# Down projection of a SwiGLU block moved to its own stage, sixteen of its inner tiles as seven block products

## The chip, the cores and the metric

The kernel runs on one core of one Trainium2 chip. The metric is the device time of one execution in microseconds (us), lower is better. A program on one core has TensorE (PE in the profile; PEld is its weight load), VectorE (DVE), ScalarE (ACT), GpSimd (POOL) and a sync engine (SP), which here issues every DMA. Each engine works through its own list of instructions in order and waits on semaphores for the others.

## The reference, cut to what matters

One layer on 1024 tokens of width 1024: a mixer (spatial gating, convolution module, gated delta rule), its output projection with a residual, and then a gated feed-forward part, which is what the change touches:

```python
x = x + jnp.einsum("bte,ed->btd", mix, w_out[l])
h = rms_norm(x, ffn_norm_g[l])
ff = jax.nn.silu(jnp.einsum("btd,df->btf", h, w_gate[l])) * jnp.einsum("btd,df->btf", h, w_up[l])
x = x + jnp.einsum("btf,fd->btd", ff, w_down[l])
return rms_norm(x, final_norm_g)
```

The inner width is 2816, which is 22 tiles of 128; all values are 32-bit floats.

## The kernel before, in words

Everything lies transposed: channels in the 128 partitions, tokens along the row, in two halves of 512. A product of 32-bit numbers is done in three passes: each operand is split into a high part (an ACT cast) and the rest (a DVE subtraction), and high x high, high x low and low x high are summed in PSUM (`PASSES`; `split_w` L126, `split` L85, `split_b` L705). So one tile of 128 x 128 weights against 512 tokens is three matmuls, and each split is one ACT and one DVE instruction of 128x512.

Gate and up (`class Matrix`, L804): two output tiles of a matrix at a time, over all eight contraction tiles. The four blocks of the weights and the four blocks of the activations (contraction halves by token halves) are combined so that seven block products take the place of eight. Each block product is 4 contraction tiles x 3 passes = 12 matmuls of 512 columns. The sums of weights, s1 to s3, are made on POOL (L832 to L843) and split as w6, w5, w7, w4, w3; w1 and w2 are plain. The sums of the activations, T1 to T4, and the plain block B22 are made once, ahead of the stage, from `b0` and `b1` on DVE and POOL. Products accumulate in two or three PSUM tiles: X takes w1, w6, w7, w4 in that order and is copied out between them (c11, c12, c22), Y takes w2, Z takes w5 and w3. The 22 matrices run as g0, u0, g1, u1, ... in `seq` (L881); the next one's w1 and w2 products stand between the present one's w7 and its w4.

Down (`class Downs`, L966): gate times up of a pair of tiles is split at once (`up_out`, L948) and kept in SBUF. After every second pair the four tiles that have come together are multiplied with all of their `w_down` rows: 16 products (8 output tiles x 2 token halves) of 4 tiles x 3 passes = 12 matmuls each, PSUM tile `pd`. Each is added to the residual: load a tile of `X1d` from DRAM into `xa`, add on DVE (L982), store it again. This is done for groups 0 to 3, tiles 0 to 15. The last six tiles (`LAST` = 20 here marks the last two of them) are multiplied at the end, PSUM tile `pdl`, with the final norm behind it in pieces of 512, 256 and 256 tokens.

Order: the program text gives each instruction a priority, and the framework's scheduler builds one fixed list per engine from it when the kernel is compiled; slots of a pool (`raw` has 2 for loaded weights, the high and low parts 6 each, `kq` 4, `d` 50) are handed out in that order and make the waits. At run time nothing is reordered. DMAs go over eight lanes in turn, and SP waits for an issue whose lane is busy, or whose data is not ready, with all later ones behind it.

Of the kernel before, what the change touches and what calls it, by code (L numbers as in the profile page):

```python
# [16 lines left out]
P = 128  # L17
# [3 lines left out]
KT = 8  # L21
# [16 lines left out]
def tile_kernel(ctx: ExitStack, tc: tile.TileContext, xT, wt, wub, wv, wout, wg, wu, wd, wdl,  # L38
# [160 lines left out]
    def token_sums(parts, w, name):  # L199
        # sum over the channels, each token in a partition  # L200
# [165 lines left out]
    # sums of the decays along the rows, each on all partitions in turn  # L366
# [46 lines left out]
    # inverses of the 32 x 32 diagonal blocks, one block to a partition  # L413
# [42 lines left out]
    def prep(c):  # L456
# [10 lines left out]
        # M' = M - M L M over pairs of 32 x 32 blocks, then of 64 x 64 blocks  # L467
# [44 lines left out]
    for c in range(NC):  # L512
# [29 lines left out]
        # the output takes the place of the chunk's queries  # L542
# [66 lines left out]
    def gating():  # L609
# [119 lines left out]
    def token_scale(ps, w, name):  # L729
        # the scale of each token, along the rows  # L730
# [66 lines left out]
    # blocks: contraction halves by token halves; T1 = B12 - B11, T2 = B22 - T1, T3 = B22 - B12, T4 = B21 - T2  # L797
# [6 lines left out]
    class Matrix:  # L804
        """Columns f and f + 1 of one of the two matrices: rows A11 A12 and A21 A22."""

        def __init__(self, src, f, name):
            self.src, self.f, self.name, self.row = src, f, name, {}
# [52 lines left out]
        def product7(self):  # L861
            product(self.X, self.w7, T3, False, False)
# [4 lines left out]
        def end(self):  # L867
            product(self.X, self.w4, T4, False, True)
            product(self.Z, self.w3, B22, False, True)
            DVE.tensor_tensor(self.c12, self.Z, self.c12, op=ALU.add)  # L870

        def product3(self):
            self.W = misc(f"W{self.name}")
            product(self.W, self.w3, B22, True, True)

        def end4(self):
            product(self.X, self.w4, T4, False, True)
# [3 lines left out]
    seq = [Matrix(src, 2 * p, f"{n}{p}") for p in range(FT // 2) for src, n in ((wg, "g"), (wu, "u"))]  # L881
# [40 lines left out]
    B22 = [block([c4p.tile([P, 2, H], F32R, tag="c4", name=f"B22{i}{j}") for j in range(2)]) for i in range(2)]  # L922
    for k in range(HB):
# [4 lines left out]
    T3 = [block([cvp.tile([P, 2, H], F32R, tag="cv", name=f"T3h{i}") for i in range(2)]),  # L928
          block([cvp.tile([P, 2, H], F32R, tag="cv", name="T3l")]) + [dt(f"T3l{k}", F32R) for k in range(2)]]
# [10 lines left out]
    ff = {}  # L940

# [6 lines left out]
    def up_out(g, u):  # L948
# [4 lines left out]
        for i, hf, t in ((0, 0, g.c11), (1, 1, g.c22), (1, 0, g.c21), (0, 1, g.c12)):  # L953
            ff[f + i, hf] = split(t, f"ff{f + i}{hf}")
# [8 lines left out]
    def group_terms(gi, n, wtile):  # L963
# [205 lines left out]
```

## Time and profile before

| | us |
|---|---|
| median of three runs | 1181.55 |
| lowest and highest | 1180.44, 1182.04 |
| profiled execution, span from the first to the last instruction | 1181.6 |
| PE busy | 1154.2 (98%) |
| DVE busy | 725.5 (61%) |
| ACT busy | 453.3 (38%) |
| POOL busy | 261.9 (22%) |

The page gives no other time of the profiled execution than its span. "Busy" adds up the time in which an engine has an instruction in work. Matmuls overlap each other, so the time from one to the next is shorter than the mean time of one. The granted clock of PE is 2.4 GHz over nearly all of the span (mean 0.994).

### The profile page before, as it was taken

The page shows a single profiled execution, that of the slowest core. Times are in us where ns is not written, and L with a number is a line of the kernel's source. Part 1 is how long each engine was busy: PE and PEld are TensorE (multiplying, and loading weights), DVE is VectorE, ACT ScalarE, POOL GpSimd, SP SyncE. Part 2 cuts the span into 40 slices and gives each one's busy share as a digit, 9 for nine tenths or more (in the row PEclk, how much of TensorE's full clock was granted, in tenths as well). Part 3 has the DMA queues.
Part 4 walks back from the last instruction along what each step waited for, and adds up shares of the span by engine and source line. Part 5 has one row for each costly group of instructions (what it writes and reads, how often), then busy time and mean ns, then how long its engine had stood idle before and what let it go on. Part 6 is the DMA issues. An engine that isn't in the chain of part 4 may idle for free.

```text
span 1181.6 us, 15892 instructions
## 1 busy us (share of the span) xinstructions
PE 1154.2 (98%) x5974; PEld 952.9 (81%) x5974; DVE 725.5 (61%) x1168; ACT 453.3 (38%) x959; POOL 261.9 (22%) x212
## 2 busy tenths in 40 slices
PE   8999999999899999979999999999999999999997
PEld 6889888888688778858888888888888888888797
DVE  7699879868987657596533654355326542645523
ACT  7456561224235654445311432144204420433422
POOL 3000130010613221564110321032004201332042
PEclk9999999999999999989999999999999999999999
DMA  6235343453313455403255125512552145215312
GB/s 227 62 98 179 108 134 102 129 193 115 131 48 107 143 174 172 144 19 106 78 182 169 59 67 172 180 58 72 165 190 74 59 134 199 81 36 182 103 58 87
DMA packets 76813, 141.68 MB, mean 120 GB/s; under 512 B 15264, under 2 KB 27200, under 8 KB 76736
## 3 DMA queue, kind: packets, MB, share of 16 engines
q1 hardware_dynamic: 76736, 140.66, 36.4%
q8 instruction: 47, 0.77, 0.3%
q14 instruction: 30, 0.25, 0.1%
HBM read 102.35 MB, written 38.29 MB: 119 GB/s over the span
## 4 chain that ended last, share of the span: by engine, by line
PE 89%; DVE 5%; issue 1%; DMA 1%; POOL 1%; ACT 1%; SPq 0%; POOLq 0%; DVEq 0%; ACTq 0%
PE pd L959 15%; PE Xu L801 10%; PE Xg L801 9%; PE po L726 7%; PE pdl L959 5%; PE Zu L801 5%; PE Zg L801 4%; PE pv L227 4%; PE pq L227 4%; PE pk L227 3%; PE pg L227 2%; PE Yu L801 2%; PE Yg L801 2%; PE pu L305 2%; PE pv L602 2%
## 5 line engine op out<-in xcount | busy, mean ns | idle before, releaser
L982 DVE TENSOR_TENSOR xa<-pd,xa 128x512 f32<-128x512 f32 x64 | 44.3, 692 | 115.1 <-PE pd L959 112.7
L959 PE MATMUL pd<-ff_l,wd_h 128*128 128x512 f32 x256 | 101.1, 395 | 0.0
L959 PE MATMUL pd<-ff_h,wd_l 128*128 128x512 f32 x256 | 101.1, 395 | 0.0
L959 PE MATMUL pd<-ff_h,wd_h 128*128 128x512 f32 x256 | 100.9, 394 | 0.0
L663 DVE SCALAR_TENSOR_TENSOR ca<-cy,vec,ca 128x512 f32<-128x512 f32 x120 | 93.1, 798 | 0.5
L832 POOL TENSOR_TENSOR s1u<-u_r 128x512 f32<-128x512 f32 x11 | 19.3, 1752 | 186.4 <-DMA u_r<-in_wu_dram 186.4
L959 PEld LDWEIGHTS pd<-ff_h,wd_h 128*128 128x128 f32 x256 | 48.2, 188 | 11.5
L959 PEld LDWEIGHTS pd<-ff_l,wd_h 128*128 128x128 f32 x256 | 48.1, 188 | 11.4
L959 PEld LDWEIGHTS pd<-ff_h,wd_l 128*128 128x128 f32 x256 | 48.1, 188 | 11.3
L843 POOL TENSOR_TENSOR s2u<-u_r,s2u 128x512 f32<-128x512 f32 x11 | 18.5, 1681 | 145.9 <-DVE w6u_l L130 145.9
L129 ACT CAST wd_h<-wd_r 128x512 fp32r<-128x512 f32 x38 | 23.4, 620 | 63.2 <-PE pd L959 24.9
L130 DVE TENSOR_TENSOR wd_l<-wd_r,wd_h 128x512 fp32r<-128x512 f32 x38 | 26.0, 686 | 34.1 <-ACT wd_h L129 34.1
L824 ACT COPY c11u<-Xu 128x512 f32<-128x512 f32 x11 | 6.4, 586 | 102.6 <-PE Xu L801 102.6
L130 DVE TENSOR_TENSOR wo_l<-wo_r,wo_h 128x512 fp32r<-128x512 f32 x32 | 27.0, 854 | 23.6 <-ACT wo_h L129 23.6
L1094 DVE TENSOR_TENSOR xf<-pdl,xf 128x256 f32<-128x256 f32 (+1 forms) x24 | 12.2, 513 | 36.7 <-PE pdl L959 36.7
L788 POOL TENSOR_TENSOR sqa<-sqa,xr 128x512 f32<-128x512 f32 x13 | 18.0, 1384 | 71.0 <-ACT xr L786 43.3
L1103 POOL TENSOR_TENSOR sqf<-sqf,sqt 128x256 f32<-128x256 f32 (+1 forms) x19 | 17.9, 942 | 63.7 <-ACT sqt L1101 63.3
L865 DVE TENSOR_TENSOR c22u<-Zu,c22u 128x512 f32<-128x512 f32 x11 | 7.6, 692 | 39.7 <-ACT c22u L864 39.7
L959 PE MATMUL pdl<-ff_h,wd_h 128*128 128x256 f32 (+1 forms) x96 | 30.8, 321 | 0.0
L959 PE MATMUL pdl<-ff_h,wd_l 128*128 128x256 f32 (+1 forms) x96 | 30.5, 318 | 0.0
L959 PE MATMUL pdl<-ff_l,wd_h 128*128 128x256 f32 (+1 forms) x96 | 30.5, 317 | 0.0
L129 ACT CAST wo_h<-wo_r 128x512 fp32r<-128x512 f32 x32 | 19.6, 616 | 27.5 <-PE po L726 16.7
(492 smaller groups left out, 3509.4 us busy)
## 6 DMA issues: line engine op xcount, KB each, us to landing
xa<-X1d SPq DMA_DIRECT2D x64, 256.0 KB, 2.7
X1d<-xa SPq DMA_DIRECT2D x64, 256.0 KB, 2.1
u_r<-in_wu_dram SPq DMA_DIRECT2D x24, 512.0 KB, 3.8
g_r<-in_wg_dram SPq DMA_DIRECT2D x23, 512.0 KB, 3.7
wd_r<-in_wd_dram SPq DMA_DIRECT2D x20, 512.0 KB, 3.6
wo_r<-in_wout_dram SPq DMA_DIRECT2D x16, 512.0 KB, 3.9
xr<-in_xT_dram SPq DMA_DIRECT2D x16, 256.0 KB, 3.7
X1d<-x SPq DMA_DIRECT2D x16, 256.0 KB, 3.2
```

What stands on the lines that cost most here:

```text
L129: ACT.copy(hi, raw)
L130: DVE.tensor_tensor(lo, raw, f32(hi), op=ALU.subtract)
L227: proj.last = PE.matmul(ps[hf], lhsT=cols(wtile, a, kt * P), rhs=(xh, xl)[b][kt][hf], start=(kt == 0 and a + b == 0), stop=(kt == KT - 1 a ...
L305: PE.matmul(ps[:, 0:264], lhsT=a[kt][hf][:, i * P:(i + 1) * P], rhs=b[:, o:o + 264], start=(kt == 0 and a is xh and b is hi), stop=(kt == ...
L602: PE.matmul(ps[:, 0:256], lhsT=a[kt][hf][:, i * P:(i + 1) * P], rhs=b[:, o:o + 256], start=(kt == 0 and a is xh and b is hi), stop=(kt == ...
L663: DVE.scalar_tensor_tensor(o, y(m), w(m), o, op0=ALU.mult, op1=ALU.add)
L726: out_mm.last = PE.matmul(ps, lhsT=cols(wtile, a, kt * P), rhs=mix[hf][kt][b], start=(kt == 0 and a + b == 0), stop=(kt == 3 and a == 1))
L801: PE.matmul(ps, lhsT=w[a][:, k * P:(k + 1) * P], rhs=blk[b][k], start=(first and k == 0 and a + b == 0), stop=(last and k == HB - 1 and a ...
L832: POOL.tensor_tensor(self.s1, a21, a22, op=ALU.add)
L843: (eng or POOL).tensor_tensor(self.s2, self.row[0][:, H:], self.s2, op=ALU.subtract)
L959: PE.matmul(ps[:, 0:cs.stop - cs.start], lhsT=cols(wtile, a, c), rhs=ff[f, hf][b][:, cs], start=(first and i + a + b == 0), stop=(last and ...
L982: DVE.tensor_tensor(xa, ps, xa, op=ALU.add)
```

## The change

The tiles of gate times up are no longer split and kept but stored to a DRAM tensor `FFd`. `Downs` goes. When gate and up are through, the down product runs as a stage of its own: tiles 0 to 15 in two groups of eight, each group four matrices of class `Down` (two output tiles each) by the same seven products, and tiles 16 to 21 plain, at the end, as before. A group (`class Group`) loads its 16 raw tiles `fr` (8 tiles x 2 token halves) and builds its own blocks B11, B21 (`fb`), T1, T2, T3, T4 (`fT1`, `fT2`, `T3`, `fT4`) and B22 from them, while the matrix before it is being multiplied and during its own first matrix. The residual is added inside `Down`, with four loads and four stores of `X1d` per matrix and two POOL additions. `LAST` becomes 16.

```diff
-            ff[f + i, hf] = split(t, f"ff{f + i}{hf}")
+            nc.sync.dma_start(FFd[f + i, hf], t)
+    class Down(Matrix):
+        def begin(self, mid=None):
+            n = self.name
+            self.X, Y = mm_ps(f"X{n}"), aux(f"Y{n}")
+            self.x11, self.x12 = self.acc(0, 0), self.acc(0, 1)
+            product(self.X, self.w1, self.blk["B11"], True, False)
+            c = dt(f"c11{n}")
+            ACT.copy(c, self.X)
+            product(Y, self.w2, self.blk["B21"], True, True)
+            DVE.tensor_tensor(self.x11, Y, self.x11, op=ALU.add)
+            POOL.tensor_tensor(self.x11, self.x11, c, op=ALU.add)
+            self.put(0, 0, self.x11)
...
+        def end(self):
+            product(self.X, self.w4, self.blk["T4"], False, True)
+            DVE.tensor_tensor(self.x21, self.X, self.x21, op=ALU.add)
+            self.put(1, 0, self.x21)
+            product(self.Z, self.w3, self.blk["B22"], False, True)
+            DVE.tensor_tensor(self.x12, self.Z, self.x12, op=ALU.add)
+            self.put(0, 1, self.x12)
+    class Group:
+        def first_rows(self, n):
+            src = self.raw[0][n * HB:(n + 1) * HB]
+            bt = self.blk[("B11", "B21")[n]] = [
+                block([kqp.tile([P, HB, H], F32R, tag="kq", name=f"fb{self.gi}{n}{i}")]) for i in range(2)]
+            for k in range(HB):
+                split_b(bt, k, src[k])
+        def t1(self):
+            b0, b1 = self.raw
+            T = self.blk["T1"] = [[None] * HB for i in range(2)]
+            for k in range(HB):
+                (POOL if k % 2 else DVE).tensor_tensor(b0[k], b1[k], b0[k], op=ALU.subtract)
+                split_d(T, k, b0[k], f"fT1{self.gi}")
...
+        def t3(self):
+            b0, b1 = self.raw
+            T = self.blk["T3"] = tiles_t3(f"f{self.gi}")
+            B = self.blk["B22"] = tiles_b22(f"f{self.gi}")
+            for k in range(HB):
+                POOL.tensor_tensor(b1[k], b1[HB + k], b1[k], op=ALU.subtract)
+                split_b(T, k, b1[k])
+            for k in range(HB):
+                split_b(B, k, b1[HB + k])
+        def t4(self):
+            b0, b1 = self.raw
+            T = self.blk["T4"] = [[None] * HB for i in range(2)]
+            for k in range(HB):
+                POOL.tensor_tensor(b0[HB + k], b0[HB + k], b0[k], op=ALU.subtract)
+                split_d(T, k, b0[HB + k], f"fT4{self.gi}")
-    class Downs:
...
     for i, m in enumerate(seq):
...
+        if i > 0:
             m.product6()
+            if new:
+                new.first_rows(0)
             m.product5()
+            if new:
+                new.first_rows(1)
         m.product7()
+        if new:
+            new.t1()
...
         elif i >= 3:
             first(nxt)
+        if new:
+            new.t2()
...
             m.end()
+        if new:
+            new.t3()
+            new.t4()
...
+    last_tiles()
+    for k in range(6):
+        load_late(LAST + k, 1)
+    for k in (4, 5):
+        split_late(LAST + k, 0)
+    for k in range(6):
+        split_late(LAST + k, 1)
+    opened += [open_late(n) for n in (1, 2, 3)]
```

Up to the first stored pair, every engine's list is the same in both kernels. Three places where the lists differ follow.

POOL, from the sums of u10 (the last matrix of gate and up) on. Before, only the squares of the final norm (`sqf`) come behind them:

```order
L832 TENSOR_TENSOR s1u10_9216<-u101_r_9214 128x512
L833 TENSOR_TENSOR s2u10_9217<-s1u10_9216,u100_r_9175 128x512
L834 TENSOR_TENSOR s3u10_9218<-u100_r_9175,u101_r_9214 128x512
L843 TENSOR_TENSOR s2u10_9217<-u100_r_9175,s2u10_9217 128x512
L1103 TENSOR_TENSOR sqf0_9492<-sqf0_9492,sqt50_9510 128x512
```

Now, the last rows ahead of the weight sums of d00, the first `Down` matrix (its name is d, group, first output tile), and the sums themselves:

```order
L1052 TENSOR_TENSOR fr010_7487<-fr051_7645,fr010_7487 128x512
L1069 TENSOR_TENSOR fr050_7643<-fr050_7643,fr010_7487 128x512
L1069 TENSOR_TENSOR fr040_7639<-fr040_7639,fr000_7483 128x512
L1052 TENSOR_TENSOR fr030_7495<-fr071_7653,fr030_7495 128x512
L1069 TENSOR_TENSOR fr070_7651<-fr070_7651,fr030_7495 128x512
L1069 TENSOR_TENSOR fr060_7647<-fr060_7647,fr020_7491 128x512
L999 TENSOR_TENSOR xad0000_8034<-xad0000_8034,c11d00_8050 128x512
L836 TENSOR_TENSOR s1d00_8087<-d000_r_8020,d001_r_8022 128x512
L837 TENSOR_TENSOR s2d00_8088<-s1d00_8087,d000_r_8020 128x512
L838 TENSOR_TENSOR s3d00_8089<-d000_r_8020 128x512
L847 TENSOR_TENSOR s2d00_8088<-d001_r_8022,s2d00_8088 128x512
```

Between s3u10 and s1d00 stand 14 rows: twelve subtractions on the group's tiles, the last sum of u10 and one addition to the residual.

DVE, at the same place. Before, between two matrices of weights stand at most the additions of the down product, here in group 3:

```order
L982 TENSOR_TENSOR xa361_8577<-pd361_8564,xa361_8577 128x512
L982 TENSOR_TENSOR xa370_8594<-pd370_8581,xa370_8594 128x512
L982 TENSOR_TENSOR xa371_8611<-pd371_8598,xa371_8611 128x512
L130 TENSOR_TENSOR w6u8_l_8663<-s2u8_8657,w6u8_h_8662 128x512
L130 TENSOR_TENSOR w5u8_l_8667<-s1u8_8656,w5u8_h_8666 128x512
```

Now, the rows ahead of the low part of d00's w6:

```order
L1052 TENSOR_TENSOR fr020_7491<-fr061_7649,fr020_7491 128x512
L90 TENSOR_TENSOR fT200_l_8069<-fr000_7483,fT200_h_8068 128x512
L998 TENSOR_TENSOR xad0000_8034<-Yd00_8033,xad0000_8034 128x512
L90 TENSOR_TENSOR fT201_l_8074<-fr010_7487,fT201_h_8073 128x512
L90 TENSOR_TENSOR fT202_l_8079<-fr020_7491,fT202_h_8078 128x512
L966 TENSOR_TENSOR c21g10_7936<-Xu10_7850,c21g10_7936 128x512
L90 TENSOR_TENSOR fT203_l_8084<-fr030_7495,fT203_h_8083 128x512
L708 TENSOR_TENSOR B22f010_8146<-fr041_7641,B22f000_8144 128x512
L708 TENSOR_TENSOR T3lf00_8142<-fr021_7493,T3hf01_8140 128x512
L131 TENSOR_TENSOR w6d00_l_8094<-s2d00_8088,w6d00_h_8093 128x512
```

From the first row on `fb00` to w6d00_l, that one included, DVE has 39 rows; 34 read two tiles in SBUF, and five read one in PSUM (c11u10, c12g10, c22u10, xad0000, c21g10). From there to w2d02_l there are 17 more, two of them with PSUM.

SP, ahead of the last weights. Before, the residual tiles `xf` are read well ahead of them:

```order
L999 DMA xf10_9317<-X1d_3858 128x512
L135 DMA wd4_r_9335<-in_wd_dram 128x1024
L135 DMA wd6_r_9345<-in_wd_dram 128x1024
L135 DMA wdl1_r_9452<-in_wdl_dram 128x1024
L135 DMA wd0_r_9462<-in_wd_dram 128x1024
```

Now the last matrix, d16, still has residual tiles to store and read back, and raw tiles to load:

```order
L988 DMA X1d_3858<-xad1601_9294 128x512
L1082 DMA fr181_9540<-FFd_5080 128x512
L1107 DMA xf01_9517<-X1d_3858 128x512
L1082 DMA fr191_9542<-FFd_5080 128x512
L1107 DMA xf11_9519<-X1d_3858 128x512
L1082 DMA fr201_9544<-FFd_5080 128x512
L1082 DMA fr211_9546<-FFd_5080 128x512
L136 DMA wdl0_r_9619<-in_wdl_dram 128x1024
```

The store of xad1601 waits for the last product of d16, and the second `xf11` for that store; wdl0 is behind both.

## Rows read from the trace of the kernel before

**Rows 1.** The page: busy time and share of PE, and the chain's shares by engine.

```profile
PE 1154.2 (98%) x5974; PEld 952.9 (81%) x5974; DVE 725.5 (61%) x1168; ACT 453.3 (38%) x959; POOL 261.9 (22%) x212
...
PE 89%; DVE 5%; issue 1%; DMA 1%; POOL 1%; ACT 1%; SPq 0%; POOLq 0%; DVEq 0%; ACTq 0%
```

**Rows 2.** Windows: busy us and instructions of each engine in two stretches.

```profile
core 0: us, PE busy (x) PEld busy (x) DVE busy (x) ACT busy (x) POOL busy (x), PEclk, DMA share, GB/s
501.00:515.00 14.00, 7.26 (x32) 5.55 (x30) 14.00 (x12) 8.19 (x16) 13.08 (x8) 0.87 0.07 30
...
1050.00:1089.00 39.00, 39.00 (x170) 31.59 (x169) 19.75 (x28) 15.18 (x28) 12.10 (x8) 1.00 0.29 97
```

**Rows 3.** Waits of PE, the longest: us in total, times, longest.

```profile
PE Xg L801 <- ACT c11g L824: 6.9, 1, 6.9
```

**Rows 4.** Chain of waits near the end, one product: start us, us, what.

```profile
1084.98 2.79 PE Zg L801 x12
```

**Rows 5.** Timeline of DVE, two additions of the down product, 12 matmuls apart.

```profile
976.45 0.69 DVE L982 TENSOR_TENSOR xa<-pd,xa 128x512 f32<-128x512 f32 x1 [2.10 <-PE pd L959]
...
979.25 0.69 DVE L982 TENSOR_TENSOR xa<-pd,xa 128x512 f32<-128x512 f32 x1 [0.86 <-PE pd L959]
```

**Rows 6.** Timeline of DVE while POOL is idle.

```profile
518.19 0.68 DVE L130 TENSOR_TENSOR w7g_l<-s3g,w7g_h 128x512 fp32r<-128x512 f32 x1
518.80 0.68 DVE L130 TENSOR_TENSOR w4g_l<-g_r,w4g_h 128x512 fp32r<-128x512 f32 x1
```

**Rows 7.** Timeline of POOL while DVE is idle.

```profile
1019.29 1.30 POOL L834 TENSOR_TENSOR s3g<-g_r 128x512 f32<-128x512 f32 x1
```

**Rows 8.** Timeline of DVE while POOL is busy.

```profile
505.15 1.12 DVE L89 TENSOR_TENSOR T_l<-x,T_h 128x512 fp32r<-128x512 f32 x1
506.19 1.77 DVE L919 TENSOR_TENSOR x<-x,x 128x512 f32<-128x512 f32 x1
507.88 1.76 DVE L89 TENSOR_TENSOR T_l<-x,T_h 128x512 fp32r<-128x512 f32 x1
509.57 0.73 DVE L748 SCALAR_TENSOR_TENSOR x<-x,vec,rwx 128x512 f32<-128x512 f32 x1
```

**Rows 9.** Timeline of POOL in the same stretch.

```profile
507.37 1.73 POOL L931 TENSOR_TENSOR x<-x,x 128x512 f32<-128x512 f32 x1
509.06 1.72 POOL L937 TENSOR_TENSOR x<-x,x 128x512 f32<-128x512 f32 x1
```

**Rows 10.** Timeline of ACT, the cast of w6 in a steady matrix.

```profile
1040.97 0.62 ACT L129 CAST w6u_h<-s2u 128x512 fp32r<-128x512 f32 x1
```

**Rows 11.** Timeline of PE after its longest wait.

```profile
515.19 0.80 PE L801 MATMUL Xg<-T_h,w6g_h 128*128 128x512 f32 x1 [6.92 <-ACT c11g L824]
...
516.63 0.63 PE L801 MATMUL Xg<-T_h,w6g_h 128*128 128x512 f32 x1
517.06 0.63 PE L801 MATMUL Xg<-T_l,w6g_h 128*128 128x512 f32 x1
```

**Rows 12.** DMA issues: KB each, median us from issue to landing.

```profile
xa<-X1d SPq DMA_DIRECT2D x64, 256.0 KB, 2.7
X1d<-xa SPq DMA_DIRECT2D x64, 256.0 KB, 2.1
...
wdl_r<-in_wdl_dram SPq DMA_DIRECT2D x2, 512.0 KB, 3.5
```

**Rows 13.** Timeline of SP: loads of weights, and eight issues in a row.

```profile
1024.87 2.08 SPq L135 DMA_DIRECT2D u_r<-in_wu_dram  x2
...
1079.23 4.96 SPq L996 DMA_DIRECT2D xf<-X1d  x8
```

**Rows 14.** Timeline of POOL, the sum for w6 of the same matrix.

```profile
1032.82 1.63 POOL L833 TENSOR_TENSOR s2u<-s1u,u_r 128x512 f32<-128x512 f32 x1
```

**Rows 15.** Timeline of DVE, a gating of the pair before.

```profile
1030.89 0.68 DVE L952 TENSOR_TENSOR c12g<-c12g,c12u 128x512 f32<-128x512 f32 x1
```

More of the change, by code (lines that the diff above doesn't have):

```diff
@@ L829, in sums @@
             n = self.name
-            a11, a12, a21, a22 = (self.row[i][:, j * H:(j + 1) * H] for i in range(2) for j in range(2))
+            a11, a12, a21, a22 = (self.part(i, j) for i in range(2) for j in range(2))
             self.s1, self.s2, self.s3 = (dt(f"s{i}{n}") for i in range(1, 4))
@@ L873, in product3 @@
             self.W = misc(f"W{self.name}")
[L874 removed]
+            product(self.W, self.w3, self.blk["B22"], True, True)
         def end4(self):
[L877 removed]
+            product(self.X, self.w4, self.blk["T4"], False, True)
             for ps in (self.Z, self.W):
                 DVE.tensor_tensor(self.c12, ps, self.c12, op=ALU.add)
[L881 removed]
+    ffn = {"B11": B11, "B21": B21}
+    seq = [Matrix(src, 2 * p, f"{n}{p}", ffn) for p in range(FT // 2) for src, n in ((wg, "g"), (wu, "u"))]
     def first(m, mid=None):
         m.load(0)
+        if isinstance(m, Down):
+            m.load(1)
         m.weights12()
@@ L888, in rest @@
     def rest(m, both=False):
-        for i in range(0 if both else 1, 2):
+        for i in range(0 if both else 2 if isinstance(m, Down) else 1, 2):
             m.load(i)
@@ L921, in tile_kernel @@
     seq[3].begin()
-    B22 = [block([c4p.tile([P, 2, H], F32R, tag="c4", name=f"B22{i}{j}") for j in range(2)]) for i in range(2)]
+    B22 = ffn["B22"] = tiles_b22("")
     for k in range(HB):
@@ L927, in tile_kernel @@
     m.begin()
-    T3 = [block([cvp.tile([P, 2, H], F32R, tag="cv", name=f"T3h{i}") for i in range(2)]),
-          block([cvp.tile([P, 2, H], F32R, tag="cv", name="T3l")]) + [dt(f"T3l{k}", F32R) for k in range(2)]]
+    T3 = ffn["T3"] = tiles_t3("")
     for k in range(HB):
@@ L940, in tile_kernel @@
     ff = {}
+    FFd = dram.tile([FT, 2, P, H], F32, name="FFd")
     def gate_out(g):
@@ L956, in down, with load_late, split_late @@
+    groups = [Group(gi) for gi in range(LAST // GROUP)]
+    opener = {}
+    for gr in groups:
+        opener[len(seq)] = gr
+        seq += [Down(wd[2 * gr.gi:2 * gr.gi + 2], n, f"d{gr.gi}{n}", gr.blk) for n in range(0, KT, 2)]
+    raws = {}
+    def load_late(f, hf):
+        raws[f, hf] = dt(f"fr{f}{hf}")
+        nc.sync.dma_start(raws[f, hf], FFd[f, hf])
+    def split_late(f, hf):
+        ff[f, hf] = split(raws[f, hf], f"ff{f}{hf}")
     def down(ps, terms, hf, first=True, last=True, cs=slice(0, H)):
@@ L1033, in tile_kernel @@
             m.end()
-        if i % 2 == 0:
-            gate_out(m)
-            g = m
-        else:
-            up_out(g, m)
-        if d is not None:
-            d.run(15)
-            first(nxt)
-            rest(nxt)
-    opened += [open_late(n) for n in (5, 6, 7)]
+        if new:
+            new.t3()
+            new.t4()
+        if i < FT:
+            if i % 2 == 0:
+                gate_out(m)
+                g = m
+            else:
+                up_out(g, m)
+    last_tiles()
+    for k in range(6):
+        load_late(LAST + k, 1)
+    for k in (4, 5):
+        split_late(LAST + k, 0)
+    for k in range(6):
+        split_late(LAST + k, 1)
+    opened += [open_late(n) for n in (1, 2, 3)]
     def load_d(src, name):
```

144 lines of the change are left out of this document (84 added, 60 removed).

## The prediction

> **What bounds the kernel now.** I read the page's busy shares and the chain of waits first: PE is busy for 98% of the span and holds 89% of the chain [rows 1], so a matmul taken away is time gained, as long as nothing makes PE wait. The waits of PE come next: the longest is one of 6.9 us [rows 3], at the opening of gate and up, where the activation blocks T1 to T4 are made. Windows show that stretch beside a steady one: in 501 to 515 us DVE is busy for 14.0 of 14 us and POOL for 13.1, PE for 7.3; in 1050 to 1089 (two matrices, 2 x 7 products) PE is busy throughout, DVE for 19.8 of 39 us and POOL for 12.1 [rows 2]. The reader is to see that the steady stage is PE's, and that making blocks is DVE's and POOL's. The change takes work from the first kind and does the second kind twice more. The timelines then give the prices of single instructions.
>
> **Matmuls.** A product of 12 matmuls takes 2.79 us in gate and up [rows 4] and 2.80 in the down stage [rows 5]. Before, tiles 0 to 15 cost 4 x 16 = 64 such products; now 2 groups x 4 matrices x 7 = 56. Eight fewer, at 2.79: 22.3 us. PE's list is shorter by just these 96 matmuls, so the change does what it says. The last six tiles have the same matmuls as before.
>
> **What goes at nothing.** 44 splits of gated tiles and 64 additions of 'pd' leave ACT and DVE inside stretches where these have half their time free [rows 2], so they give nothing back. Inside a group a Down matrix has 12 DVE instructions (some 8 us) and 6 on POOL (10 us at the dearest, 1.7 each) for 19.5 us of PE: covered. The transfers rise from 128 to 152 of 256 KB; if SP's list were late with weights, it would cost what the second rival says.
>
> **The price of two instructions at once.** Alone, DVE starts a 128x512 subtraction of two SBUF tiles every 0.6 us [rows 6], POOL takes 1.3 [rows 7]. Where both have work, DVE's take 1.77 and 1.76 and POOL's 1.73 and 1.72, each starting 1.69 us after the one before [rows 8, 9]: they take turns, and one DVE plus one POOL instruction cost 1.69, so a turn of POOL costs DVE 1.69 - 0.6 = 1.09 us. DVE instructions that read PSUM keep their 0.73 beside a busy POOL [rows 8]. An ACT cast takes 0.62 [rows 10]; ACT is busy for 8.2 of the 14 us [rows 2] and not the one that is late.
>
> The Trainium skill, "SBUF — State Buffer", section "Who interferes with whom", says that a DVE instruction with two SBUF inputs and a GpSimd instruction that reads SBUF exclude each other for the whole instruction. The turns agree with it, their sum not quite: fully blocked, a turn of POOL would cost DVE 1.3 instead of the 1.09 of the rows, and by that the total below would be 8.6 us higher, 1197.3. I keep the rows.
>
> **The first opening.** Take t = 0 at the start of u10's w6 product, a product as 2.78 (39.0 us for 14 of them in rows 2). Without a wait d00's w6 product would start after seven products, at 19.5, and d00's last (w3) would end after 14, at 38.9. The splits `fb` go into the slots of the old B11, free when u10's w1 product ends, three products ahead of t = 0; with one cast DVE can start at -8.3 + 0.6 = -7.7. From there to w6d00_l DVE has 34 instructions with two SBUF tiles (20.4 us) and five that read PSUM and run beside POOL. POOL has 17 by then: twelve subtractions for T1 to T4, s2u10, the addition to xad0000, s1, s2 and s3 of d00, at 1.09 each 18.5 us. For waits of the two on each other (c12g10 and c22u10 need PE) I add 0.9, one turn: -7.7 + 20.4 + 18.5 + 0.9 = 32.1, where PE wants w6 at 19.5. Its first two matmuls need only the high part, a little earlier; that changes nothing, because DVE goes on being late: up to w2d02_l, which the second matrix's w2 product needs before d00's w4 and w3 can run, come 15 more with SBUF (9.0), two with PSUM (1.2) and three turns of POOL (3.3): 45.6. PE then has 10 + 12 + 12 matmuls left, 7.9 us, and ends at 53.5. Lost: 53.5 - 38.9 = 14.6 us.
>
> **The second opening** (d06 into d10) has the same shape: 32 with SBUF and 19 turns of POOL (19.2 + 20.7), so w6d10_l at -7.7 + 39.9 + 0.9 = 33.1; then 13 (7.8), two with PSUM (1.2) and two turns (2.2): 44.3; PE ends at 52.2. Lost: 13.3 us. Queued behind the late instructions are the residual additions on DVE and the loads of d02's and d12's weights on SP; the latter wait for s3 of the matrix before and land in time by 512 KB's 3.5 us [rows 12].
>
> No row of before shows this very mix. The bounds are a turn of POOL at 0.44 (the 1.12 us instruction, which starts the next 1.04 us after itself, where POOL had begun during a PSUM read [rows 8]) and at 1.3 (nothing overlaps [rows 7]). With 17 + 3 + 19 + 2 = 41 turns the two openings together, 27.9 us at 1.09, lie between 1.3 and 36.5. I take 1.09, because both engines have a backlog throughout, as in rows 8 and 9.
>
> **The end.** The store of d16's last residual tile waits for its last product; the load of the same tile waits for that store, and wdl0 is behind it on SP. From the end of that product: 0.2 of signals (estimate), addition 0.7, store 2.1 [rows 12], four issues at 4.96 / 8 = 0.62 [rows 13], landing 3.5, cast 0.6: 9.6 us for the high part, 10.3 for the low. PE has three products, 8.4. Lost: 1.5 us, between 0 (a quicker store) and 4 (a load at twice 3.5).
>
> **Sum**, on the profiled execution's 1181.6 (the page shows nothing around its span, and the median of the runs is 0.05 lower): 1181.6 - 22.3 + 14.6 + 13.3 + 1.5 = 1188.7.
>
> **Rivals.**
> First, the other side, faster: a turn of POOL is cheaper than 1.09, because many of them fall beside DVE's PSUM reads or its waits. The 1.12 us row speaks for it, rows 2 (two engines full for 14 us while PE waits) against it. The point from which it decides: the openings may cost 22.3 - 1.5 = 20.8, so 41 turns have to be 0.17 cheaper, 0.92 us each. Halfway to the bound, at 0.77, the openings cost 14.8 and the time is 1175.6; at the bound it is 1162.1.
> Second, more is lost: after 6.9 us of waiting PE's matmuls start 0.43 us apart instead of 0.23 for some seven instructions, at the lower clock of 1.2 GHz [rows 11]; here that would come after two gaps in each opening, 4 x 1.4 = 5.6. To it come the residual loads of d02, which stand on SP behind eight raw tiles of the next group and a store that waits for c12g10: if they land some 3 us after DVE reaches them, each opening loses that again. Against it: in the first gap the slow matmuls lie beside a DVE that is later still. 1188.7 + 5.6 + 6 = 1200.3.
> Third, gate and up get waits of their own, since stores of gated tiles now stand on SP ahead of loads of weights. In a steady matrix of before the loads of weights are out by 1027.0 [rows 13]; the store in front of them would wait for a gating that ends at 1031.6 [rows 15], 4.6 us later. The sum for w6 is ready at 1034.5 [rows 14] and its cast starts at 1041.0 [rows 10], so 6.5 us are spare and I expect nothing. Were it 2 us too late in each of eight pairs, the time would be 1204.7.
>
> **How the numbers follow.** The forecast has a chance of 0.60 and spans 1180 to 1196 by a turn between 0.88 and 1.27; the first rival 0.25, the second 0.11, the third 0.04. A measurement of this kernel tells 0.2%, 2.4 us, from no change: 1179.2 to 1184.0. Faster: 0.22 of the first rival and 0.01 of the forecast's lower end, 0.23. Same: 0.03 and 0.08, 0.11. Slower: the rest, 0.66. The range is 1172 to 1200: down to a turn of 0.68, up to the second rival; the forecast's own is the 1180 to 1196 above.
>
> **What would show it.** Right: PE busy falls by some 22 us and the span rises; two stretches of about 45 us, at u10/d00 and d06/d10, where DVE and POOL are both full, with DVE's two-SBUF instructions at 1.0 to 1.8 us; PE's longest waits there, 10 us or so each, on w6 and w1 or w2 of the Down matrices, and nearly none inside a group. The pdl products with wdl0 wait 1 to 2 us. Wrong: PE full through the openings, or the waits ending on DMA, or waits spread over gate and up.

## The result, and the profile after

The changed kernel takes 1209.0 us (median of four runs, 1206.9 to 1211.9); the kernel before took 1181.2 in the same rounds (1180.4 to 1182.0). The ratio is 1.0229, with a 95% interval of 1.0207 to 1.025. The forecast was slower, 1188.7 (1172 to 1200): the direction was right, the size was not, and the time lies outside the range. The profiled execution took 1208.42, its span is 1206.6, 25.0 more than before.

The page of the changed kernel, the lines that answer to [rows 1]:

```profile
PE 1144.1 (95%) x5878; PEld 941.4 (78%) x5878; DVE 785.0 (65%) x1200; ACT 489.4 (41%) x1023; POOL 376.0 (31%) x284
...
PE 74%; DVE 10%; DMA 5%; POOL 5%; issue 3%; ACT 1%; SPq 1%; POOLq 0%; DVEq 0%; ACTq 0%
```

There are 96 matmuls fewer, and PE's share of the chain fell from 89% to 74%: a quarter of the span is now set by others. An opening is the stretch in which a group's blocks are made, from u10 into d00 and from d06 into d10. Windows, in the columns of [rows 2], of the first opening (two rows), the second (two rows) and a steady pair of Down matrices:

```profile
906.00:938.00 32.00, 21.53 (x85) 16.69 (x83) 30.88 (x31) 13.42 (x25) 20.77 (x14) 0.86 0.25 82
938.00:965.00 27.00, 24.00 (x87) 18.74 (x88) 19.58 (x25) 10.86 (x20) 12.86 (x8) 0.85 0.57 195
...
1005.00:1042.00 37.00, 22.09 (x86) 17.27 (x85) 34.63 (x33) 12.69 (x23) 26.23 (x17) 0.86 0.24 85
1042.00:1064.00 22.00, 20.94 (x84) 16.47 (x83) 18.39 (x24) 10.21 (x18) 10.35 (x8) 0.93 0.57 180
1064.00:1103.00 39.00, 39.00 (x169) 31.58 (x169) 19.16 (x25) 10.65 (x18) 16.93 (x12) 1.00 0.50 170
```

The steady pair is as cheap as forecast: PE busy throughout, 39 us for 14 products. The openings look as forecast in their first part (DVE nearly full, PE idle for a third and more), but PE's granted clock is 0.86 there. PE's waits, which before had one long entry [rows 3]:

```profile
PE Xd L802 <- ACT w6d_h L130: 16.1, 2, 8.1
PE Xd L802 <- DVE xad L1004: 8.9, 2, 6.8
PE Xg L802 <- ACT c11g L828: 6.9, 1, 6.9
PE pdl L1090 <- ACT wdl_h L89: 3.7, 1, 3.7
PE Xu L802 <- ACT c12u L863: 2.9, 1, 2.9
```

The first and the fourth were forecast (the fourth as 1 to 2), and the third is the one of before. The second and the fifth were not: PE's product w7 waits for the engine that reads X out after w6.

How the loss is measured. In a stage that loses nothing, the first matmul of one matrix's w6 product comes 19.5 us (seven products) after that of the matrix before. PE's timeline gives these starts; the first three around u10, d00 and d02:

```profile
906.04 0.40 PE L802 MATMUL Xu<-T_h,w6u_h 128*128 128x512 f32 x1
...
938.40 0.80 PE L802 MATMUL Xd<-fT_h,w6d_h 128*128 128x512 f32 x1 [7.99 <-ACT w6d_h L130]
...
964.38 0.39 PE L802 MATMUL Xd<-fT_h,w6d_h 128*128 128x512 f32 x1
```

So the first two steps took 32.4 and 26.0 us. The table has the same starts from one profiled execution of each kernel; the experiments follow below. From u10 to d04 are three steps with the first opening, from d04 to d14 four steps with the second. The end runs from d14's w6, the last matrix but one, to the end of the span; for the kernel before it is one step of 19.5 and the 94.0 us behind u10's w6.

| | u10 to d04 | d04 to d14 | to the end | median us |
|---|---|---|---|---|
| without loss | 58.5 | 78.0 | 113.5 (before) | 1181.2 (before) |
| after | 79.4 | 98.1 | 123.0 | 1209.0 |
| e1_xact | 85.6 | 101.3 | 121.4 | 1218.3 |
| e2_dve | 79.8 | 94.2 | 123.7 | 1205.3 |
| e3_noopen | 58.5 | 78.0 | 122.8 | 1170.1 |
| e4_tail | 81.2 | 98.6 | 117.2 | 1205.5 |
| e5_later | 76.0 | 94.8 | 121.2 | 1202.8 |
| e7_presub_tail | 72.4 | 91.7 | 116.7 | 1192.2 |
| e8_warm | 85.3 | 101.2 | 120.8 | 1219.4 |
| e9_s4 | 71.9 | 90.5 | 115.9 | 1187.7 |
| e10_raw3 | 78.4 | 87.8 | 113.3 | 1193.6 |
| e11_order | 64.6 | 93.7 | 115.5 | 1183.7 |
| e12_spread | 63.6 | 88.9 | 115.1 | 1175.9 |
| e13_spread3 | 62.2 | 85.4 | 113.1 | 1175.5 |

The changed kernel loses 20.9 and 20.1 us in the openings and 9.5 at the end. Gate and up lose nothing (their steps are 19.4 and 19.5). The mixer ended 3.0 us earlier than in the profiled execution of before (the matmul of [rows 11] at 515.19 is at 512.15 now; in the other profiled executions below it lies between 512.5 and 519.2, so that two of them can differ by some us ahead of the stage). 1181.6 - 22.3 + 20.9 + 20.1 + 9.5 - 3.0 = 1206.8, against a span of 1206.6.

### The profile page after: what moved, and what is told of

Its sections match the earlier page's. It is cut to its first block, busy times and chain, and to the rows that moved or that the text cites. A ratio compares the mean times of both kernels' runs of the same rounds, so it can differ in the third digit from the quotient of the medians.

```text
span 1206.6 us, 15998 instructions
## 1 busy us (share of the span) xinstructions
PE 1144.1 (95%) x5878; PEld 941.4 (78%) x5878; DVE 785.0 (65%) x1200; ACT 489.4 (41%) x1023; POOL 376.0 (31%) x284
## 4 chain that ended last, share of the span: by engine, by line
PE 74%; DVE 10%; DMA 5%; POOL 5%; issue 3%; ACT 1%; SPq 1%; POOLq 0%; DVEq 0%; ACTq 0%
PE Xu L802 10%; PE Xg L802 9%; PE po L727 7%; PE pdl L1090 5%; PE Zu L802 4%; PE Zg L802 4%; PE pv L228 4%; PE pq L228 4%; PE pk L228 3%; PE Xd L802 2%; PE pg L228 2%; PE Yu L802 2%; PE Yg L802 2%; PE pu L306 2%; PE pv L603 2%
## 5 line engine op out<-in xcount | busy, mean ns | idle before, releaser
L131 DVE TENSOR_TENSOR wo_l<-wo_r,wo_h 128x512 fp32r<-128x512 f32 x32 | 25.9, 819 | 23.8 <-ACT wo_h L130 23.7
L789 POOL TENSOR_TENSOR sqa<-sqa,xr 128x512 f32<-128x512 f32 x13 | 17.7, 1360 | 71.9 <-ACT xr L787 44.4
L836 POOL TENSOR_TENSOR s1g<-g_r 128x512 f32<-128x512 f32 x11 | 14.5, 1319 | 68.5 <-DMA g_r<-in_wg_dram 62.4
L869 DVE TENSOR_TENSOR c22g<-Zg,c22g 128x512 f32<-128x512 f32 x11 | 7.6, 691 | 43.1 <-ACT c22g L868 43.1
L847 POOL TENSOR_TENSOR s2g<-g_r,s2g 128x512 f32<-128x512 f32 x11 | 18.1, 1642 | 56.2 <-DVE w6g_l L131 56.2
L1012 POOL TENSOR_TENSOR xad<-xad,c22d 128x512 f32<-128x512 f32 x8 | 10.8, 1350 | 69.3 <-ACT c22d L1010 46.3
L130 ACT CAST wo_h<-wo_r 128x512 fp32r<-128x512 f32 x32 | 19.6, 616 | 27.2 <-PE po L727 15.6
L90 DVE TENSOR_TENSOR fT_l<-fr,fT_h 128x512 fp32r<-128x512 f32 x24 | 28.9, 1219 | 1.7 <-ACT fT_h L89 1.6
L802 PE MATMUL Xd<-fT_h,w6d_h 128*128 128x512 f32 x32 | 14.1, 442 | 16.1 <-ACT w6d_h L130 16.1
L802 PE MATMUL Xg<-b,w1g_h 128*128 128x512 f32 x88 | 27.6, 395 | 0.0
L802 PE MATMUL Yu<-b,w2u_h 128*128 128x512 f32 x88 | 27.6, 395 | 0.0
L802 PE MATMUL Xu<-b,w1u_h 128*128 128x512 f32 x88 | 27.6, 395 | 0.0
L802 PE MATMUL Yg<-b,w2g_h 128*128 128x512 f32 x88 | 27.5, 394 | 0.0
```

The source lines that it names most:

```text
L90: DVE.tensor_tensor(lo, src, f32(hi), op=ALU.subtract)
L130: ACT.copy(hi, raw)
L131: DVE.tensor_tensor(lo, raw, f32(hi), op=ALU.subtract)
L802: PE.matmul(ps, lhsT=w[a][:, k * P:(k + 1) * P], rhs=blk[b][k], start=(first and k == 0 and a + b == 0), stop=(last and k == HB - 1 and a ...
L836: POOL.tensor_tensor(self.s1, a21, a22, op=ALU.add)
L847: (eng or POOL).tensor_tensor(self.s2, self.part(0, 1), self.s2, op=ALU.subtract)
```

## The experiments

Each kernel is the changed one with the edit shown. Before, in the same rounds, was between 1182.1 and 1183.0.

**e3_noopen: no blocks are made, and their raw tiles are not loaded.**

```diff
-            self.gi, self.blk, self.raw = gi, {}, [[None] * GROUP for hf in range(2)]
+            self.gi, self.blk, self.raw = gi, ffn, [[None] * GROUP for hf in range(2)]
...
-        new = opener.get(i + 1)
+        new = None
...
-        elif i + 4 in opener or i + 3 in opener:
+        elif False:
```

> Leaves out the building of the group blocks: both groups multiply with the activation blocks of gate and up (and the loads of the sixteen raw tiles go), so the down product's values are not the reference's; matmuls, weights, residual and the end are as in the changed kernel. Theory A, the two openings lose 19.4 + 20.2 us and nothing else in the stage loses much: 1209.0 - 39.6 = 1169 (1166 to 1173). Theory B, of the loss only the forecast's 27.9 us is the making of blocks and the rest belongs to the stage itself (residual tiles on DRAM, waits on X, weights behind stores): 1181 (1178 to 1184).

Measured 1170.1 (ratio 0.9902, 0.9886 to 0.9919). Theory A: every step of the stage is 19.5, so the 39 us belong to the blocks, that is to their making and to the loads of their raw tiles, which this kernel leaves out together. The stores of the tiles and the residual through DRAM are still there and cost the stage nothing. PE's longest waits are the one at the opening of gate and up, as before, and one at the end:

```profile
PE Xg L802 <- ACT c11g L828: 6.9, 1, 6.9
PE pdl L1090 <- ACT wdl_h L89: 4.2, 1, 4.2
```

**e4_tail: SP's order at the end.**

```diff
+    for k in (4, 5):
+        split_late(LAST + k, 0)
+    wl = load_d(wdl[0], "wdl0")
     last_tiles()
...
-    wl = load_d(wdl[0], "wdl0")
```

> The load of the first piece of the last weights (wdl0) is written ahead of the loads of the residual tiles xf and of the raw tiles of the second token half; SP has it before the last three stores of d16. Theory A, the end loses 3.7 us of wait on wdl0 and some 2.8 us of half clock behind it because of SP's order: 1203 to 1204. Theory D, the end is bound by the splits and by the late wd0 and wd2, and the wait only changes its name: 1208 to 1209.

Measured 1205.5 (1.0196, 1.0181 to 1.0211), 3.5 below the changed kernel; the end took 5.8 us less (theory A), and the profiled execution lost 3.9 of them again ahead of it, 1.7 before u10 and 2.2 in the openings. The intervals of this ratio and of the changed kernel's overlap, so that the end is shorter rests on the traces. SP and PE after, then in e4_tail:

```profile
1121.58 0.32 SPq L988 DMA_DIRECT2D X1d<-xad  x1
...
1123.20 0.32 SPq L988 DMA_DIRECT2D X1d<-xad  x1
...
1128.18 0.38 SPq L136 DMA_DIRECT2D wdl_r<-in_wdl_dram  x1
...
1134.53 0.80 PE L1090 MATMUL pdl<-ff_h,wdl_h 128*128 128x512 f32 x1 [3.69 <-ACT wdl_h L89]
1135.12 0.63 PE L1090 MATMUL pdl<-ff_l,wdl_h 128*128 128x512 f32 x1
```

```profile
1116.92 0.33 SPq L136 DMA_DIRECT2D wdl_r<-in_wdl_dram  x1
...
1134.48 0.39 PE L1090 MATMUL pdl<-ff_h,wdl_h 128*128 128x512 f32 x1
1134.71 0.39 PE L1090 MATMUL pdl<-ff_l,wdl_h 128*128 128x512 f32 x1
```

With the load out 11 us sooner PE does not wait, and the 24 matmuls with wdl0 take 5.6 us from first start to last end instead of 8.6, those of the changed kernel starting 0.43 us apart at first: the wait had cost its length and nearly as much again in clock.

**e1_xact: the reader of X moved to ACT.**

```diff
-            DVE.tensor_tensor(self.x12, self.X, self.x12, op=ALU.add)
+            c = dt(f"c12{self.name}")
+            ACT.copy(c, self.X)
+            DVE.tensor_tensor(self.x12, c, self.x12, op=ALU.add)
```

> In Down.product6 the PSUM tile X is now read by an ACT copy, and DVE adds the copy to the residual later; everything else as in the changed kernel (median 1209.0). Theory A, the openings lose three things, the backlog of DVE and POOL, PE's wait for the reader of X before the w7 product, and half clock behind each gap: PE's wait for DVE's xad (8.9 us in two places) goes, w7 of d06 starts some 4 to 5 us earlier (ACT has the copy behind casts of w1 and w2 of d10, whose weights land around then), the second opening shortens by about 3 to 5 us: 1204 to 1206. Theory B, the backlog of DVE alone sets the end of an opening (the low part of w2 of the group's second matrix), and the wait on X only lies inside it: PE waits the same time elsewhere, 1208 to 1209.

Measured 1218.3 (1.0305, 1.029 to 1.032): slower by 9, which neither theory said. In the profiled execution 4.1 us of that lie ahead of u10, and the openings are 9.4 us longer. The wait for DVE's xad is gone, and in its place d06's w7 waits 4.7 us for the copy, which stands on ACT behind a cast whose weights are not there (the step from d06 to d10 is 1.3 us shorter, 35.2):

```profile
1024.59 0.62 ACT L130 CAST w2d_h<-d_r 128x512 fp32r<-128x512 f32 x1 [2.76 <-DMA d_r<-in_wd_dram]
1025.12 0.58 ACT L1005 COPY c12d<-Xd 128x512 f32<-128x512 f32 x1
```

The loss is in the steps behind (27.3 us from d02 to d04, 23.8 from d12 to d14): DVE reaches the next addition in its list before the residual tile has landed, and PE's w3 waits for the Z that this addition reads.

```profile
981.79 0.69 DVE L1013 TENSOR_TENSOR xad<-Zd,xad 128x512 f32<-128x512 f32 x1 [6.66 <-DMA xad<-X1d]
```

**e2_dve: all subtractions on DVE.**

```diff
-                (POOL if k % 2 else DVE).tensor_tensor(b0[k], b1[k], b0[k], op=ALU.subtract)
+                DVE.tensor_tensor(b0[k], b1[k], b0[k], op=ALU.subtract)
```

(and the same for T2, T3, T4)

> All sixteen subtractions that form T1 to T4 of a group stand on DVE (twelve were on POOL). Theory A, DVE and POOL take turns, so a POOL turn costs DVE 1.09 us: an opening loses 12 x 1.09 of turns and gains 12 x 0.6 of work on DVE, 5.9 us less, and the sums for w6 on POOL no longer stand behind six turns of subtractions: 10 to 14 us faster than the changed kernel, 1195 to 1199. Theory C, POOL's work runs mostly beside DVE's and DVE's own instructions are the bill: 12 x 0.6 more in each opening, 1216 to 1223.

Measured 1205.3 (1.0192, 1.0172 to 1.0212), 3.7 below the changed kernel, with overlapping intervals of the ratios. Theory C is out, and A is right for the waits on w6 only: w6 of d00 starts 26.1 us after u10's instead of 32.4, and that of d10 27.8 after d06's instead of 36.5, but the first opening ends no sooner (79.8 for 79.4), and the second 3.9 us sooner (94.2 for 98.1). What is late next, in the first opening, is a residual tile; its load stands on SP behind the raw tiles of the next group:

```profile
955.52 0.69 DVE L1011 TENSOR_TENSOR xad<-Zd,xad 128x512 f32<-128x512 f32 x1 [7.82 <-DMA xad<-X1d]
```

```profile
946.29 4.29 SPq L1032 DMA_DIRECT2D fr<-FFd  x7
950.62 1.85 SPq L984 DMA_DIRECT2D xad<-X1d  x4
```

**e5_later: e2_dve with the raw loads one matrix later.**

```diff
-        elif i + 4 in opener or i + 3 in opener:
+        elif i + 3 in opener or i + 2 in opener:
```

> As e2_dve, with the loads of each group's sixteen raw tiles one matrix later, so that group 1's stand on SP behind the residual loads of the first opening. Theory E, in e2_dve the residual tiles landed 7.8 and 7.1 us after DVE reached them because SP had eight raw loads in front, and DVE, in order, held the weights behind them: these two waits go, the steps from d00's w6 to d04's w6 (28.9 + 24.9 us there, 39.0 without loss) fall by 8 to 12, 1193 to 1198. Theory F, the residual loads wait for their own slots or for data, not for SP's order: 1203 to 1207.

Measured 1202.8 (1.0174, 1.0154 to 1.0194), 2.6 below e2_dve, whose own runs lie between 1202.0 and 1207.9. Theory E for the cause (the 7.8 us wait is gone, and the first opening is 3.8 us shorter), but not for the size: a matrix later DVE still waits 3.8 us for a residual tile, and the second opening is no shorter (94.8 for 94.2).

**e8_warm: small matmuls in PE's waits.**

```diff
+            if i in (22, 26):
+                keep_warm(33)
             m.product6()
...
+        if i in (21, 22, 25):
+            keep_warm({21: 10, 22: 8, 25: 28}[i])
         m.product7()
```

> As the changed kernel, with small extra matmuls (128 columns, on constants, into an unused PSUM tile) in PE's list in five of its waits: 10 ahead of u10's w7, 33 ahead of d00's w6, 8 ahead of d00's w7, 28 ahead of d06's w7, 33 ahead of d10's w6, each sized from rows of the changed kernel to end before the wait does. Theory A, the half clock behind each gap (a product of 4.2 to 4.5 us for 2.8) is lost time: the granted clock stays high behind them and the time falls by 3 to 7 us, 1202 to 1206. Theory B, the slow matmuls lie beside DVE and POOL that are later still: 1208 to 1210.

Measured 1219.4 (1.0324, 1.0296 to 1.0353): slower by 10. In the first part of both openings the granted clock stays at 1.00 (0.86 in the same two windows after), and u10's w7, d00's w6 and d06's w7 start their matmuls 0.23 us apart, where it was 0.43. In the second part it does not: d00's w7 from its seventh matmul on and d10's w6 from its third are 0.43 apart, and the clock from d00's w6 to d02's and from d10's to d12's is 0.94 and 0.88 (0.84 and 0.91 after). First parts, then second parts, columns as above:

```profile
900.00:950.00 50.00, 46.09 (x249) 38.74 (x247) 43.41 (x51) 26.00 (x48) 30.93 (x18) 1.00 0.22 74
1000.00:1050.00 50.00, 47.84 (x268) 40.72 (x266) 44.67 (x42) 20.17 (x38) 36.89 (x24) 1.00 0.25 81
...
941.00:969.00 28.00, 23.64 (x102) 19.00 (x103) 17.11 (x24) 10.85 (x20) 10.37 (x8) 0.94 0.62 216
...
1048.00:1076.00 28.00, 23.52 (x86) 18.29 (x87) 19.06 (x26) 11.40 (x21) 11.47 (x8) 0.88 0.41 139
```

The two steps in whose stretch no engine's list differs but PE's show what that is worth: from u10's to d00's w6 nothing (32.6 for 32.4; theory B), from d06's to d10's 1.7 us (34.8 for 36.5). From d00's w7 on the order on DVE and SP differs as well (the addition that frees X stands behind a split, residual loads behind stores), and the steps behind the two gaps are longer (27.5, 25.2 and 27.3 for 26.0, 21.1 and 22.6). So the clock costs nothing as far as w6 of d00; what it costs behind that, and over the whole stage, stays open.

**e7_presub_tail: the subtractions moved out of the openings.** With e4_tail's edit. Behind each pair's gating:

```diff
+        for k, a, b, t in rows:
+            if l < HB:
+                DVE.tensor_tensor(t, b, a, op=ALU.subtract)
+                nc.sync.dma_start(Td[1, gi, k], t)
+            else:
+                t1, b12 = dt(f"q1{f}{k}"), dt(f"q3{f}{k}")
+                nc.sync.dma_start(t1, Td[1, gi, k])
+                nc.sync.dma_start(b12, FFd[GROUP * gi + k, 1])
+                DVE.tensor_tensor(t1, b, t1, op=ALU.subtract)
...
```

> The sixteen subtractions T1 to T4 of each group are done on DVE right behind the gating of each pair, in the gate and up stage, and stored to DRAM; an opening loads B11, B21, B22 and T1 to T4 raw (28 tiles instead of 16) and only splits them. With e4_tail's order at the end. Theory A, the openings lose the subtractions and their turns with POOL: w6's low part then comes at -7.7 + 30 x 0.6 + 5 x 1.09 = 15.8 us at the latest, before PE wants it at 19.5, so both gaps on w6 go and an opening loses 0 to 5 us; with e3_noopen's 1170.0 and e4_tail's gain of 3.5 to 5.7: 1165 to 1176. Theory F, the openings are bound by the transfers and SP's order, which now carry 12 tiles more: each still loses 10 or more, 1185 to 1200.

Measured 1192.2 (1.0082, 1.0062 to 1.0103). Between the theories: the waits on w6 fall from 16.1 to 3.3 us and each opening is 6 to 7 us shorter, and gate and up keep their 19.5; what is left ends mostly on late weights and residual tiles (theory F). PE waits 6.2 us for casts of w2, and 2.4 for that of d04's w1, for whose weights ACT was idle for 11.86 us; their load left SP at 960.6, behind raw tiles of the group and stores that waited for their data:

```profile
PE Yd L802 <- ACT w2d_h L130: 6.2, 3, 2.9
...
PE Xd L802 <- ACT w6d_h L130: 3.3, 2, 1.7
PE Xd L802 <- ACT w1d_h L130: 2.4, 1, 2.4
```

```profile
966.79 0.62 ACT L130 CAST w1d_h<-d_r 128x512 fp32r<-128x512 f32 x1 [11.86 <-DMA d_r<-in_wd_dram]
```

**e9_s4, e10_raw3, e11_order: loads and slots.** All three start from e7_presub_tail. Two of the three edits of e9_s4 are shown; the third loads each group's raw tiles one matrix later. e10_raw3 adds a third slot for weights (`bufs=3`, and 49 small tiles), e11_order places the loads anew:

```diff
+        def sums(self):
+            super().sums()
+            self.s4 = dt(f"s4{self.name}")
+            POOL.tensor_tensor(self.s4, self.part(0, 1), self.s2, op=ALU.subtract)
...
+        def weights3(self, eng=None):
+            self.w3 = split_w(self.s4, f"w3{self.name}")
...
-            POOL.tensor_tensor(self.x11, self.x11, c, op=ALU.add)
+            DVE.tensor_tensor(self.x11, self.x11, c, op=ALU.add)
```

> As e7_presub_tail, with three edits in the group stage: the sum for w3 of a Down matrix goes to a tile of its own right behind the sum for w6 (it no longer waits for the split of w6, and the raw weights come free sooner), the two residual additions on POOL stand on DVE, and each group's raw tiles are loaded one matrix later. Theory G, what is left of the openings (13.9 and 13.8 us in e7_presub_tail) is the chain by which the next matrix's raw weights come: slot free, load behind other issues on SP, cast, PE's waits on w2 and w1: those waits (6.2 and 2.4 us) mostly go, an opening loses 3 to 8, 1174 to 1186. Theory A, what is left is still DVE's backlog of 28 splits: 1190 to 1194.

> As e9_s4, with three slots for raw weights instead of two (and 49 of the small tiles instead of 50, for the room). Theory G: one of the next matrix's two loads of weights is out a product or more earlier, so the rest of the waits on w1 and w2 shrinks: 2 to 6 us below e9_s4. Theory A: the same as e9_s4 within 1.5 us; with a slot of the small tiles less, it may be up to 2 us more.

> As e9_s4; group 0's raw tiles are loaded one matrix earlier (group 1's as there), and the raw tiles of T4 and of B22 are loaded later, behind the splits of T1, so that the sums of the next matrix's weights get their tiles sooner; on DVE the low part of w6 then stands ahead of the splits of B22 and T3's second half. Theory G (the order of loads and tiles, not the amount of work, is what is left): in the first opening the 11.0 us wait for w6 of d00, which followed raw tiles that landed 9 us late, falls to under 3, and the second opening loses 6 to 9 instead of 11.7: 1174 to 1181, level with the kernel before (1182.6) or faster. Theory A (DVE's 28 splits beside two matrices' own work fill its time): the first opening falls as said, the second stays at 11 to 12: 1179 to 1184.

e9_s4: 1187.7 (1.0034, 1.0014 to 1.0055), between the theories. The waits on w1 and w2 went, as theory G said, but the raw tiles, now a matrix later, came too late for group 0. ACT was idle for 9.04 us for them, ahead of the cast of w6 in its list, and PE waited 11.0 for that cast:

```profile
936.01 0.62 ACT L707 CAST B22f<-rB 128x512 fp32r<-128x512 f32 x1 [9.04 <-DMA rB<-FFd]
```

```profile
PE Xd L802 <- ACT w6d_h L130: 11.0, 1, 11.0
```

e10_raw3: 1193.6 (1.0092, 1.0075 to 1.0109), slower than e9_s4, a miss for both theories: with that same late load the second opening is shorter (87.8 for 90.5), the first longer (78.4 for 71.9). e11_order: 1183.7 (1.001, 0.9993 to 1.0026), level with before. The first opening loses 6.1; the second 15.7, more than either theory said: PE waits 4.26 us there for the cast of d12's w1, whose weights left SP at 1021.7, and on DVE all splits of T4 and B22 stand ahead of the low parts of w1 and w2.

**e12_spread, e13_spread3: the last splits behind the next weights.**

```diff
             first(nxt)
+            if i in opener:
+                opener[i].make("T4")
+                opener[i].make("B22")
...
-            for t in ("T3", "T4", "B22"):
-                new.make(t)
+            new.make("T3")
```

> As e11_order, with the splits of T4 and B22 written into the group's own first matrix, behind the w1 and w2 products of the next one: only the blocks of the first five products are made in the matrix before. Theory G, what is left (6.2 and 15.6 us in e11_order) is work that stands ahead of more urgent work on DVE: the low parts of w1 and w2 of the second matrix come some 4 to 5 us earlier against the splits, each opening loses 2 to 4 us less, 1176 to 1181. Theory A, DVE's work as a whole fills the opening, and an order that favours one thing delays another: 1182 to 1185.

> As e12_spread, with three slots for raw weights (and 49 small tiles). Theory G: in e11_order the loads of d12's weights left SP at 1021.7, right behind the low part of w4 of d10 that frees the slot; with a third slot the first of the two loads goes a matrix earlier: another 2 to 4 us, 1172 to 1178, faster than the kernel before. Theory A: no difference from e12_spread beyond 1.5 us.

e12_spread: 1175.9 (0.994, 0.9927 to 0.9954), theory G by the time, and faster than both kernels; the second opening is 4.8 us shorter than in e11_order, the first 1.0. e13_spread3: 1175.5 (0.9936, 0.9921 to 0.9951), theory A by the time. Its openings are 4.9 us shorter than e12_spread's, but in its profiled execution the mixer ends 6 us later (the matmul of [rows 11] stands at 519.2 and 513.0); why stays open. PE's waits of the group stage in e12_spread are short:

```profile
PE Xd L802 <- DVE w6d_l L131: 3.0, 2, 1.8
...
PE Xd L802 <- ACT w1d_h L130: 2.4, 2, 1.2
PE Xd L802 <- ACT c22d L1038: 2.0, 2, 1.3
```

## Why the prediction was wrong in size

**Matmuls, steady matrices, gate and up**: right. 96 matmuls left PE's list, every steady step outside the openings is 19.4 to 19.6 apart from d02 to d04 (21.1), and the third rival fails.

**The price of turns**: right. In the first opening DVE and POOL take 1.70 us a pair, a DVE read of PSUM 0.68, as in [rows 8, 9]:

```profile
926.40 1.77 DVE L1052 TENSOR_TENSOR fr<-fr,fr 128x512 f32<-128x512 f32 x1
928.10 1.78 DVE L90 TENSOR_TENSOR fT_l<-fr,fT_h 128x512 fp32r<-128x512 f32 x1
929.80 0.68 DVE L998 TENSOR_TENSOR xad<-Yd,xad 128x512 f32<-128x512 f32 x1
```

The low part of w6 of d00 was forecast to be done 32.1 us after u10's w6 and was done at 938.38 + 1.55 - 906.04 = 33.9; that of w2 of d02 was forecast at 45.6 and was done at 952.12 + 0.68 - 906.04 = 46.8. Both are a little late, so the first rival (cheaper turns) is out. By the Trainium skill, "SBUF — State Buffer", "Who interferes with whom", a pair excludes each other for the whole instruction; the trace agrees that they take turns but not with the full price, since a pair takes 1.70 where 0.6 and 1.3 [rows 6, 7] would make 1.9.

That these marks came out within 2 us does not mean that DVE's own list was the path: w6's high part waited for POOL's sum, which stood behind the subtractions, and both lists ended together. POOL, then ACT:

```profile
932.65 1.70 POOL L999 TENSOR_TENSOR xad<-xad,c11d 128x512 f32<-128x512 f32 x1
934.32 1.70 POOL L836 TENSOR_TENSOR s1d<-d_r 128x512 f32<-128x512 f32 x1
936.10 1.59 POOL L837 TENSOR_TENSOR s2d<-s1d,d_r 128x512 f32<-128x512 f32 x1
```

```profile
937.73 0.62 ACT L130 CAST w6d_h<-s2d 128x512 fp32r<-128x512 f32 x1 [6.71 <-POOL s2d L837]
```

**The step that failed** is the one behind these marks: "PE then has 10 + 12 + 12 matmuls left, 7.9 us". It supposed that PE had done w7, and the next matrix's w1, by then. PE had not, because w7 accumulates into X, and X is read after w6 by DVE, in order, behind its backlog. The prediction named these additions as queued behind the late instructions and did not ask which matmul waits for them. In the second opening, DVE and then PE:

```profile
1011.01 1.28 DVE L708 TENSOR_TENSOR fb<-fr,fb 128x512 fp32r<-128x512 f32 x2
...
1012.82 3.42 DVE L708 TENSOR_TENSOR fb<-fr,fb 128x512 fp32r<-128x512 f32 x3
1016.16 0.68 DVE L1045 TENSOR_TENSOR fr<-fr,fr 128x512 f32<-128x512 f32 x1
1016.76 0.68 DVE L1004 TENSOR_TENSOR xad<-Xd,xad 128x512 f32<-128x512 f32 x1
```

```profile
1017.59 0.76 PE L802 MATMUL Xd<-T3hf,w7d_h 128*128 128x512 f32 x1 [6.83 <-DVE xad L1004]
1018.15 0.63 PE L802 MATMUL Xd<-T3lf,w7d_h 128*128 128x512 f32 x1
1018.58 0.63 PE L802 MATMUL Xd<-T3hf,w7d_l 128*128 128x512 f32 x1
```

The wait was over before the gap on w6, but DVE and POOL need PE's products as well: the low part of w6 of d10 was done at 38.0 us after d06's w6 instead of 33.1, that of w2 of d12 at 48.6 instead of 44.3, and PE had 10.4 us left behind it instead of 7.9 (59.1 for 52.2). In the first opening w7 of d00 ended its wait at 949.97 and started at half clock (0.43 us from matmul to matmul instead of 0.23). When w2 of d02 was done PE still had the last six matmuls of that w7 and ten of w1 ahead of the 34 of the forecast, 11.5 us instead of 7.9 (58.3 for 53.5); 1.6 more went between d02 and d04. So the openings cost 41.0 instead of 27.9. That these 13 us come from the wait on X alone is argued, not shown: e1_xact took the wait away and another came in its place, and no run moves the reader of X ahead of DVE's backlog and nothing else.

**The end**: the term was mis-sized, 9.5 for 1.5. SP's queue was right as the place (e4_tail), but the load of wdl0 took 5.7 us to land (1128.18 to the cast at 1133.86) instead of 3.5, so that the wait was 3.7. The half clock behind it cost 3.0, and two waits that the sum did not have came to 1.8: d16's w4 waited 1.3 for the copy c22d, and the first product of the last tiles 0.5 for a split. Together these are 8.5 of the 9.5.

**The rivals.** The second had both of its mechanisms in the trace: slow products behind five waits, and residual tiles for which DVE waited 5.35 us (at 958.15) and 6.98 (at 975.18) while PE had other work. Its 1200.3 is still 8.7 too low. [rows 11] showed the clock term after the longest wait of before, and the forecast gave it nothing; how much of the 13 us it is stays open: 1.7 us by e8_warm behind d06's w7, and about 1.4 behind d00's w7, an estimate from its first seven starts (2.7 us from 949.97 to 952.70, where six times 0.23 are 1.4). The third rival's 1204.7 was the nearest of all the cases by luck, since gate and up, where it put the loss, lost nothing.

## What to carry to other kernels

An opening that is too full for two engines is not priced by the fuller engine's list alone: ask for each product which reader must free its PSUM tile, and what stands in front of that reader on its own engine, and on SP in front of its operand. Where every queue is in order, taking away one wait shows the next (e1_xact, e2_dve, e5_later); what paid was to take work out of the crowded stretch into one that has room (e7_presub_tail) and then to put the urgent rows first (e11_order, e12_spread), 33 us in all with the end. A seven-product scheme saves PE's time only if its sums are made where others idle: with the openings away it was worth 11 to 12 us of 22 here with the end untouched (e3_noopen, whose values are not the reference's), and 7 in the best kernels that compute them (e12_spread, e13_spread3).

## What was not expected of the hardware

With matmuls of 128 columns on constants in the waits PE's granted clock stayed at 1.00 over the first part of both openings (0.86 without), and the time was longer all the same, by 10 us, in steps where the order on other engines differs too. A wait of 3.7 us at the end cost 6.7: 24 matmuls took 8.6 us behind it and 5.6 without it.
